# One pair's fourth weight sum in its own tile, and a residual prepared by accumulating transfers, in a Trainium2 encoder trunk

## Chip, cores and metric

The kernel runs on one core of one Trainium2 chip. The metric is the device time of one execution in microseconds (us); smaller is better. The engines are called PE (TensorE), DVE (VectorE), ACT (ScalarE), POOL (GpSimd) and SP (SyncE). SP issues the weight loads from memory, POOL issues the transfers that add one tile of the on-chip memory to another, and works little otherwise.

## What is computed

Two requests of 512 and 256 tokens, 768 tokens of 1024 values, run through two layers with shared weights. Each layer is a feed-forward block (FFN), a token mixer and a second FFN; the first layer's mixer is a gated linear recurrence, the second's a windowed attention. A last normalisation ends the trunk. The part that matters here is the FFN, run four times (f0, f1 around the first mixer, f2, f3 around the second):

```python
def swiglu_ffn(x, w1, w2):              # x [768,1024], w1 [1024, 2 x 2816], w2 [2816,1024]
    gate, up = jnp.split(x @ w1, 2, axis=-1)
    return (jax.nn.silu(gate) * up) @ w2

x = x + 0.5 * swiglu_ffn(rmsnorm(x, g), w1, w2)
```

All data are float32.

## The kernel before

**Storage and precision.** x stays on chip in six tiles of 128 tokens by 1024 values; the first three are the token half 0, the last three half 1. A float32 operand is split into a high and a low part: ACT copies it into the matmul's rounded format (the high part), and DVE subtracts that from the original (the low part). A product is three matmuls, high by high, high by low, low by high. The weights are split so at L225 (ACT) and L226 (DVE), activations at L369 and L370.

**Seven products.** A pair of 128 columns of the gate matrix and the 128 of the up matrix is treated as a 2 x 2 block matrix: a11 and a12 are the upper and lower half of the gate columns, a21 and a22 those of the up columns; the tokens are the two halves. As in the Strassen-Winograd scheme seven products p1 to p7 take the place of eight, with sums of weights on one side (for p7: a21 + a11; for p3 the sum of all four blocks) and sums of activations s1 to s4 on the other. The activation sums are made on DVE by `first_sum` and `up_sums` (L503, L511). The down projection works the same way, and its results are added to x by `add_x` (L792).

**The residual trick.** The down products of a block are combined so that x can take them directly. For that the residual is prepared once per FFN: with x12, x22 the left and right half of a token block in half 1, and x21 the right half of the block in half 0, x12 += x22 and x21 -= x22. Before, that is six DVE operations (L720 and L721, three each) in `down_quad`, at the first group only, anywhere behind the last sum. They are undone at the end, in `down_last`.

**The opening.** f0 starts with two plain pairs. f1, f2 and f3 start with one plain pair (pair 0, two halves of tokens), woven with the *opened pair*, pair 1, whose products run in the order p7, p3, (plain half 1), p1, p2, p6, p5, p4, in `opened_pair` (L671). p7 needs s1 and p3 needs plain activations only, so both can start before half 1 is normalised and turned. PE meanwhile turns the normalised token blocks (L435), and ACT evicts what PE turned (L446).

**Weights.** `quad_steps` (L195) loads a pair's two raw tiles (`wr`, four buffers of 512 KB) and one block more into an `s3` tile (two buffers of 256 KB), adds a11 to that tile and a22 to a21 by accumulating transfers (`into`, L155, issued by POOL), and stages the seven weights in an order, here `OPEN`: p1, p2, p7, p3, p6, p5, p4. In an opened pair two more sums follow in place: *second* (a11 += a21) behind p1's split, and *fourth* (a12 += a11) behind p2's split and the landing of second. p3's weight is a12 after fourth. SP and POOL work through their transfers in the order of the program; a transfer that waits keeps all behind it.

Of the kernel before, what the change touches and what calls it, by code (L numbers as in the profile page):

```python
# [12 lines left out]
AF = mybir.ActivationFunctionType  # L13
# [3 lines left out]
P = 128  # L17
# [18 lines left out]
HB = H // P  # L36
PLAIN = {"f0": 2, "f1": 1, "f2": 1, "f3": 1}
# [8 lines left out]
OPEN = ("p1", "p2", "p7", "p3", "p6", "p5", "p4")  # L46
# [11 lines left out]
class Trunk:  # L58
    def __init__(self, ctx, tc, consts):
        self.tc, self.nc = tc, tc.nc  # L60
        pool = lambda name, **kw: ctx.enter_context(tc.tile_pool(name=name, bufs=1, **kw))
        self.cp = pool("consts")
        self.xp = pool("xp")
        self.wp = pool("wp")
        self.tp = pool("tp")
        self.sp = pool("stats")
        self.ap = pool("arena")
        self.pp = pool("psum", space=bass.MemoryType.PSUM)
        self.dp = pool("dram", space=bass.MemoryType.DRAM)
        self.uid = 0  # L70
        self.deferred = []
        self.queue, self.loaded, self.staged, self.held = [], [], {}, 0
        self.more = {}
        self.shut = False
        self.setup(consts)

    def name(self, s):
# [119 lines left out]
    def quad_steps(self, key, raws, srcs, order):  # L197
        nc = self.nc
        flat = lambda t: t.rearrange("p a b -> p (a b)")
        up = len(raws) == 2  # L200
        if up:
            a11, a12, a21, a22 = (flat(t[:, h : h + 4, :]) for t in raws for h in (0, 4))
            three = [srcs[1].rearrange("(k p) c -> p k c", p=P)[:, :4, :]]
        else:
            a11, a12, a21, a22 = (flat(t) for t in raws)
            three = [srcs[2][:, i : i + 1, :] for i in range(2)]
        spare = up and (PLAIN[key[0]] == 2 or key[1] > 2)
        s3 = []
        for i, src in enumerate(three):
            t = self.wp.tile([P, 512], F32, tag="s3", name=self.name("s3"), bufs=2)  # L210
            self.last_load = nc.sync.dma_start(t.rearrange("p (a b) -> p a b", a=src.shape[1]), src)
            self.into(t, a11[:, i * 512 : (i + 1) * 512])
            s3.append(t)
        self.into(a21, a22)

        def split(name, srcs, eng=None):
            if up:
                w = self.wtile()
                hi, lo = w[:, :512], w[:, 512:]
            else:  # L220
                hi, lo = self.wtile(), self.wtile()
            n = srcs[0].shape[-1]
            for i, src in enumerate(srcs):
                h, l = (t[:, i * n : (i + 1) * n] for t in (hi, lo))
                nc.scalar.copy(h, src)  # L225
                (eng or nc.vector).tensor_sub(l, src, h.bitcast(F32))  # L226
            view = lambda t: t.rearrange("p (a b) -> p a b", a=4 if up else 2)
            self.staged[(*key, name)] = (view(hi), view(lo), 1 if up else 2)

        own = {"p1": [a11], "p2": [a12], "p3": [a12], "p4": [a22], "p5": [a21], "p6": [a11], "p7": s3}  # L230
        pin = self.tc.keep_in_program_order
        add = {"second": lambda: nc.vector.tensor_add(a11, a11, a21), "fourth": lambda: nc.vector.tensor_add(a12, a12, a11)}  # L232
        before = {} if up else {"p6": "second", "p3": "fourth"}
        behind = {"p5": "second", "p4": "fourth"} if up else {}

        if order == OPEN:
            add = {"second": lambda: self.into(a11, a21), "fourth": lambda: self.into(a12, a11)}
            behind, pin = {"p1": "second", "p2": "fourth"}, lambda ins: None

        def step(name):  # L240
            if name in before:
                pin(add[before[name]]())
            split(name, own[name], nc.gpsimd if spare and name == "p5" else None)
            if name in behind:
                pin(add[behind[name]]())

        gated = lambda i: order == OPEN and i >= GATED
        return [(1 if up else 2, lambda name=name: step(name), gated(i)) for i, name in enumerate(order)]
# [240 lines left out]
    def sums(self):  # L489
        tiles = lambda kp: [self.tn[(i // 2, i % 2)][:, kp] for i in range(4)]  # L490
        third = [tiles(kp)[3] for kp in range(2)]
        for kp, t in enumerate(third):
            self.nc.vector.tensor_sub(t, tiles(kp)[1], t)
        for name, out, x, y in (("t1", 1, 0, 1), ("t2", 0, 0, 3), ("t4", 2, 2, 0)):
            for kp in range(2):
                t = tiles(kp)
                self.nc.vector.tensor_sub(t[out], t[x], t[y])
                self.put(name, kp, t[out])
        for kp, t in enumerate(third):
            self.put("t3", kp, t)  # L500
        self.last_sum = self.last_lo

    def first_sum(self):  # L503
        for kp in range(2):
# [6 lines left out]
    def up_sums(self):  # L511
        add, sub = self.nc.vector.tensor_add, self.nc.vector.tensor_sub
        for name, op, out, x, y in (
            ("s2", sub, (1, 0), (1, 0), (0, 1)),
            ("s3", sub, (0, 0), (0, 1), (0, 0)),
            ("s4", add, (1, 1), (1, 1), (1, 0)),
        ):
            for kp in range(2):
                t = self.tn[out][:, kp]
                op(t, self.tn[x][:, kp], self.tn[y][:, kp])  # L520
                self.put(name, kp, t)
        self.last_sum = self.last_lo

    def spill_factors(self):
        self.kept = {}
        for name in ("t3", "t2", "t1", "t4"):
            for kp in range(2):
                t = self.kept[(name, kp)] = self.dp.tile([P, 4 * H], F32, name=self.name("kept"))
                self.nc.gpsimd.dma_start(t, self.ops[(name, kp)].bitcast(F32).rearrange("p a b c -> p (a b c)"))
# [60 lines left out]
    def gated(self, pss, act=None, dve=None):  # L590
        t = self.tmp(H)
        with self.tc.issue_after(act) if act else nullcontext():
            self.nc.scalar.activation(t, pss[0], AF.Silu)
        with self.tc.issue_after(dve) if dve else nullcontext():
            self.nc.vector.tensor_mul(t, t, pss[1])
        return t
# [116 lines left out]
    def down_quad(self, tag, g, hid):  # L713
        nc = self.nc
        cols = lambda b, c: self.x[b][:, c * 512 : (c + 1) * 512]
        if g == 0:
            with self.tc.issue_after(self.last_sum):
                for i in range(HB):
                    x12, x21, x22 = cols(HB + i, 0), cols(i, 1), cols(HB + i, 1)
                    nc.vector.tensor_add(x12, x12, x22)  # L720
                    nc.vector.tensor_sub(x21, x21, x22)  # L721
        banks = {}
        for name in DOWN:
            wh, wl = self.take((tag, "down", g, name))
            chain = {"p2": "p1", "p4": "p5", "p3": "p7"}.get(name, name)
            for i in range(HB):
                if name == chain:
                    banks[(chain, i)] = self.ps()
                ps = banks[(chain, i)]
                sl = slice(i * P, (i + 1) * P)  # L730
                for kp in range(2):
                    h = hid[FACTOR[name]]
                    a, w = (h[:, kp, 0, sl], h[:, kp, 1, sl]), (wh[:, kp, :], wl[:, kp, :])
                    for q, (x, y) in enumerate(((0, 0), (0, 1), (1, 0))):
                        nc.tensor.matmul(  # L735
                            ps,
                            a[x],
                            w[y],
                            start=name == chain and kp == 0 and q == 0,
                            stop=kp == 1 and q == 2,  # L740
                            skip_group_check=True,
                        )
                x22 = cols(HB + i, 1)
                dst = {"p2": cols(i, 0), "p4": cols(i, 1), "p3": cols(HB + i, 0)}.get(name, x22)
                self.add_x(dst, ps, -0.5 if name in ("p1", "p5") else 0.5)
            self.done((tag, "down", g, name))
# [1004 lines left out]
```

## Time and profile before

| What | us |
|---|---|
| three runs | 2758.54, 2761.22, 2761.22 |
| median | 2761.22 |
| the profiled execution | 2758.39 |
| its span, first to last instruction | 2756.5 |
| f1's opening, roughly | 1005 to 1055 |
| f2's opening | 1500 to 1570 |
| f3's opening | 2250 to 2335 |

The rest of the page: the mean granted clock of TensorE over the span is 0.999. The transfers moved 334.41 MB, 121 GB/s in the mean. A row of the timeline gives the start, the time, the engine, the source line and operation, the kind of tile written and read, the shapes, the count of equal neighbours, and in brackets the engine's idle time before it with what released it. A row of the chain of waits gives a start, a time and what ran then on the path that ended last. Neighbouring matmuls overlap: one starts before the one ahead has ended. An ACT cast whose source is `wr` or `s` splits a weight; one whose source is `big` or `tA` splits an activation.

### The profile page before, as it was taken

To read this page: it belongs to the slowest core of one execution; us is meant where nothing else is said; L and a number is where in the kernel's file an instruction comes from. 1 tells how busy PE (TensorE), PEld (TensorE's weight loads), DVE (VectorE), ACT (ScalarE), POOL (GpSimd) and SP (SyncE) were. 2 spreads that over 40 slices of the span, in tenths; PEclk is the share of its full clock that TensorE was granted. 3 is DMA by queue.
4 is the path that set the end of the run, shared out by engine and by line. 5 is a ranking of instruction groups with operands and counts; after the bars stand their busy time and mean duration, and the time that the engine had idled before them with its cause. 6 is when DMAs were issued, how large, how long until landed. Compare 5 with 4: busy or idle time off the path is not lost.

```text
span 2756.5 us, 41004 instructions
## 1 busy us (share of the span) xinstructions
PE 2731.8 (99%) x15045; PEld 2538.8 (92%) x15045; DVE 2199.7 (80%) x3802; ACT 1404.4 (51%) x2645; POOL 459.0 (17%) x516
## 2 busy tenths in 40 slices
PE   8999999999999999999999999999999999999998
PEld 8999999989999889999998999999888889999997
DVE  8788788768887889788878977887847869788877
ACT  6444444634455675444455643444458855444443
POOL 1111121200000110211121121112005621211120
PEclk9999999999999999999999999999999999999999
DMA  6554556741122744655555365545424434655453
GB/s 171 133 127 113 124 144 166 226 140 39 39 61 64 203 121 100 145 134 125 119 135 130 92 146 133 126 118 138 130 73 114 87 65 98 144 134 130 119 130 111
DMA packets 358362, 334.41 MB, mean 121 GB/s; under 512 B 14904, under 2 KB 273424, under 8 KB 358160
## 3 DMA queue, kind: packets, MB, share of 16 engines
q1 hardware_dynamic: 305328, 226.40, 27.9%
q0 software_dynamic: 48528, 91.90, 19.2%
q10 hardware_dynamic: 4304, 13.49, 1.4%
q8 instruction: 118, 1.93, 0.3%
q14 instruction: 84, 0.69, 0.1%
HBM read 227.66 MB, written 15.73 MB: 88 GB/s over the span
## 4 chain that ended last, share of the span: by engine, by line
PE 91%; DVE 4%; ACT 2%; DMA 1%; issue 1%; POOL 0%; DVEq 0%; ACTq 0%; POOLq 0%
PE ps L626 41%; PE ps L735 16%; PE ps L768 6%; PE ps L949 6%; PE ps L364 5%; PE ps L365 5%; PE ps L366 5%; PE ps L1012 3%; DVE big L370 1%; PE ps L1117 1%; DVE w L226 1%; PE ps L1605 1%; DMA wr<-wr 1%; PE ps L435 1%; PE ps L1093 1%
## 5 line engine op out<-in xcount | busy, mean ns | idle before, releaser
L626 PE MATMUL ps<-big,w 128*128 128x384 f32 x6972 | 1214.2, 334 | 2.9 <-ACT w L225 2.4
L626 PEld LDWEIGHTS ps<-big,w 128*128 128x128 f32 x6972 | 1209.3, 188 | 5.3 <-ACT w L225 2.7
L225 ACT CAST w<-wr 128x512 fp32r<-128x512 f32 (+1 forms) x618 | 430.5, 704 | 665.7 <-PE ps L626 315.3
L226 DVE TENSOR_TENSOR w<-wr,w 128x512 fp32r<-128x512 f32 (+1 forms) x541 | 435.2, 808 | 143.1 <-ACT w L225 121.8
L735 PE MATMUL ps<-w,big 128*128 128x512 f32 x2016 | 461.1, 390 | 0.2 <-DVE x L796 0.2
L735 PEld LDWEIGHTS ps<-w,big 128*128 128x128 f32 x2016 | 376.6, 188 | 80.6 <-ACT big L369 2.7
L155 POOL DMA_DIRECT2D s<-wr x129 | 113.6, 887 | 1248.0 <-DVE wr L232 362.4
L796 DVE SCALAR_TENSOR_TENSOR x<-ps,x 128x512 f32<-128x512 f32 x420 | 273.1, 683 | 12.8 <-PE ps L768 12.4
L370 DVE TENSOR_TENSOR big<-tA,big 128x384 fp32r<-128x384 f32 x308 | 190.3, 629 | 20.5 <-ACT big L369 20.3
L155 POOL DMA_DIRECT2D wr<-wr x118 | 104.0, 881 | 549.7 <-DVE big L370 152.1
L369 ACT CAST big<-tA 128x384 fp32r<-128x384 f32 x308 | 152.7, 514 | 81.2 <-DVE tA L667 30.4
L364 PE MATMUL ps<-big,w 128*128 128x384 f32 x544 | 187.5, 345 | 0.8 <-ACT w L191 0.8
L365 PE MATMUL ps<-big,w 128*128 128x384 f32 x544 | 183.1, 337 | 0.1
L366 PE MATMUL ps<-big,w 128*128 128x384 f32 x544 | 182.7, 336 | 0.0
L949 PE MATMUL ps<-w,big 128*128 128x512 f32 x756 | 178.1, 393 | 0.1
L768 PE MATMUL ps<-w,big 128*128 128x512 f32 x756 | 174.6, 391 | 0.9 <-DVE x L796 0.9
L768 PEld LDWEIGHTS ps<-w,big 128*128 128x128 f32 x756 | 141.0, 188 | 31.0 <-DVE x L796 2.1
L949 PEld LDWEIGHTS ps<-w,big 128*128 128x128 f32 x756 | 140.3, 188 | 28.9 <-DVE w L370 0.6
L226 POOL TENSOR_TENSOR w<-wr,w 128x512 fp32r<-128x512 f32 x77 | 111.7, 1451 | 104.5 <-ACT w L225 102.0
L232 DVE TENSOR_TENSOR wr<-wr,wr 128x512 f32<-128x512 f32 (+1 forms) x120 | 109.8, 915 | 0.0
L654 DVE TENSOR_TENSOR tA<-tA,ps 128x384 f32<-128x384 f32 x80 | 44.0, 550 | 81.0 <-PE ps L626 81.0
L364 PEld LDWEIGHTS ps<-big,w 128*128 128x128 f32 x544 | 102.3, 188 | 1.3 <-ACT w L191 1.1
(234 smaller groups left out, 3691.7 us busy)
## 6 DMA issues: line engine op xcount, KB each, us to landing
wr<-in_ffn_w_dram SPq DMA_DIRECT2D x256, 512.0 KB, 4.0
s<-wr POOLq DMA_DIRECT2D x129, 256.0 KB, 4.7
s<-in_ffn_w_dram SPq DMA_DIRECT2D x123, 256.0 KB, 3.2
wr<-wr POOLq DMA_DIRECT2D x89, 256.0 KB, 4.1
wr<-in_hg_w_in_dram SPq DMA_DIRECT2D x32, 512.0 KB, 3.9
wr<-wr POOLq DMA_DIRECT2D x29, 512.0 KB, 4.6
spill<-x ACTq DMA_DIRECT2D x12, 512.0 KB, 3.9
kept<-big POOLq DMA_DIRECT2D x8, 768.0 KB, 6.5
```

The lines of the kernel that those rows point to most:

```text
L155: self.nc.gpsimd.dma_start(out, src, accum_op=ALU.add)
L225: nc.scalar.copy(h, src)
L226: (eng or nc.vector).tensor_sub(l, src, h.bitcast(F32))
L364: nc.tensor.matmul(out, a[0], b[0], start=first, stop=False)
L365: nc.tensor.matmul(out, a[0], b[1], start=False, stop=False)
L366: nc.tensor.matmul(out, a[1], b[0], start=False, stop=last)
L370: self.last_lo = self.nc.vector.tensor_sub(lo, src, hi.bitcast(F32)).ins
L626: self.nc.tensor.matmul(ps, a[x], b[y], start=first and k == 0 and i == 0, stop=k == 3 and i == 2, skip_group_check=True,)
L735: nc.tensor.matmul(ps, a[x], w[y], start=name == chain and kp == 0 and q == 0, stop=kp == 1 and q == 2, skip_group_check=True,)
L768: nc.tensor.matmul(ps, a[x], w[y], start=name == chain and k == 0 and q == 0, stop=k == 2 and q == 2, skip_group_check=True,)
L796: self.nc.vector.scalar_tensor_tensor(x, ps, c, x, ALU.mult, ALU.add)
L949: nc.tensor.matmul(ps, x[:, sl], y, start=fresh and k == 0 and q == 0, stop=k == 3 and q == 2, skip_group_check=True,)
```

## The change

Two things change in f1, f2 and f3; f0 and the mixers keep their code.

1. The opened pair gets a second `s3` tile. It is loaded with a12, a11 is added to it, and then a21 once a22 has been added to that. p3 takes its weight from this tile. The transfer *fourth* is gone; *second* stays. Both `s3` buffers are now taken by the opened pair, until p7 and p3 have been split.
2. `up_sums`, right behind s2, calls a new `prepare`: for each of the three token blocks an ACT copy with the factor -1 makes -x22 in a scratch tile, and two accumulating transfers do x12 += x22 and x21 += -x22. `down_quad` does its DVE work in f0 only.

```diff
-            three = [srcs[1].rearrange("(k p) c -> p k c", p=P)[:, :4, :]]
+            part = lambda i, k: srcs[i].rearrange("(k p) c -> p k c", p=P)[:, k : k + 4, :]
+            three = [part(1, 0)] + ([part(0, 4)] if order == OPEN else [])
...
-            self.into(t, a11[:, i * 512 : (i + 1) * 512])
+            self.into(t, a11 if up else a11[:, i * 512 : (i + 1) * 512])
             s3.append(t)
         self.into(a21, a22)
+        if order == OPEN:
+            self.into(s3[1], a21)
...
         if order == OPEN:
-            add = {"second": lambda: self.into(a11, a21), "fourth": lambda: self.into(a12, a11)}
-            behind, pin = {"p1": "second", "p2": "fourth"}, lambda ins: None
+            own.update({"p3": s3[1:], "p7": s3[:1]})
+            add = {"second": lambda: self.into(a11, a21)}
+            behind, pin = {"p1": "second"}, lambda ins: None
...
                 self.put(name, kp, t)
+            if name == "s2" and self.joined:
+                self.prepare()
         self.last_sum = self.last_lo
+        self.joined = True
+
+    def prepare(self):
+        cols = lambda b, c: self.x[b][:, c * 512 : (c + 1) * 512]
+        neg = self.big([P, HB, 512])
+        for i in range(HB):
+            x12, x21, x22 = cols(HB + i, 0), cols(i, 1), cols(HB + i, 1)
+            self.nc.scalar.activation(neg[:, i], x22, AF.Copy, scale=-1.0)
+            self.into(x12, x22)
+            self.into(x21, neg[:, i])
...
-        if g == 0:
+        if g == 0 and PLAIN[tag] == 2:
```

`joined` is False until `up_sums` has run for the first time, which is in f0.

How the instructions move is told at three places. The first is POOL in f1, from the opened pair's first accumulation on. Before (1278 is p7's tile, 1276 holds a11 and a12, 1277 a21 and a22, 1313 to 1315 belong to pair 2, 1357 to 1359 to pair 3):

```order
L155 DMA s3_1278_8967<-wr_1276_8963 128x512
L155 DMA wr_1277_8965<-wr_1277_8965 128x512
L155 DMA s3_1315_9208<-wr_1313_9204 128x512
L155 DMA wr_1314_9206<-wr_1314_9206 128x512
L155 DMA wr_1276_8963<-wr_1277_8965 128x512
L155 DMA wr_1276_8963<-wr_1276_8963 128x512
L155 DMA s3_1359_9475<-wr_1357_9471 128x512
```

and now (1279 is p3's tile, 1314 to 1316 are pair 2's, 1359 to 1361 pair 3's, 1245 to 1247 the three x tiles of half 1, 1230 an x tile of half 0, 1352 the scratch tile):

```order
L155 DMA s3_1278_8967<-wr_1276_8963 128x512
L155 DMA s3_1279_8970<-wr_1276_8963 128x512
L155 DMA wr_1277_8965<-wr_1277_8965 128x512
L155 DMA s3_1279_8970<-wr_1277_8965 128x512
L155 DMA wr_1315_9210<-wr_1315_9210 128x512
L155 DMA x_1245_8771<-x_1245_8771 128x512
L155 DMA x_1246_8773<-x_1246_8773 128x512
L155 DMA wr_1276_8963<-wr_1277_8965 128x512
L155 DMA x_1247_8775<-x_1247_8775 128x512
L155 DMA s3_1316_9212<-wr_1314_9208 128x512
L155 DMA s3_1361_9488<-wr_1359_9484 128x512
L155 DMA x_1230_8685<-big_1352_9430 128x512
```

The two sums into p3's own tile come ahead of everything, fourth (`wr_1276<-wr_1276`) is gone, and pair 2's p7 sum has moved from ahead of second to behind it.

The second place is ACT in f1, where p7's weight is split. Before, from p7's cast (w_1325) to p3's (w_1326):

```order
L225 CAST w_1325_9283<-s3_1278_8967 128x512
L446 ACTIVATE big_1329_9309<-ps_1328_9305,cols_92 128x384
L446 ACTIVATE big_1329_9309<-ps_1330_9311,cols_92 128x384
L446 ACTIVATE big_1329_9309<-ps_1331_9316,cols_92 128x384
L446 ACTIVATE big_1329_9309<-ps_1332_9321,cols_92 128x384
L369 CAST big_1333_9326<-big_1329_9309 128x2x384
L369 CAST big_1334_9329<-big_1329_9309 128x2x384
L446 ACTIVATE big_1336_9345<-ps_1335_9341,cols_92 128x384
L446 ACTIVATE big_1336_9345<-ps_1337_9347,cols_92 128x384
L446 ACTIVATE big_1336_9345<-ps_1338_9352,cols_92 128x384
L225 CAST w_1326_9286<-wr_1276_8963 128x512
```

and now:

```order
L228 CAST w_1326_9286<-s3_1278_8967 128x512
L228 CAST w_1327_9289<-s3_1279_8970 128x512
L450 ACTIVATE big_1330_9312<-ps_1329_9308,cols_92 128x384
L450 ACTIVATE big_1330_9312<-ps_1331_9314,cols_92 128x384
L450 ACTIVATE big_1330_9312<-ps_1332_9319,cols_92 128x384
L450 ACTIVATE big_1330_9312<-ps_1333_9324,cols_92 128x384
```

p3's cast has moved up over nine instructions and stands ahead of the first evictions. Further on, behind s2's first halves, ACT now has the three copies (the second of s2's casts ahead, s3's and s4's casts behind, then p4's weight, pair 2's p1 weight and the eviction of plain half 1's bank, once L686, now L701):

```order
L373 CAST big_1351_9427<-big_1306_9181 128x2x384
L535 ACTIVATE big_1352_9430<-x_1245_8771 128x512
L535 ACTIVATE big_1352_9430<-x_1246_8773 128x512
L535 ACTIVATE big_1352_9430<-x_1247_8775 128x512
L373 CAST big_1353_9441<-big_1295_9129 128x2x384
L373 CAST big_1354_9445<-big_1295_9129 128x2x384
L373 CAST big_1355_9449<-big_1337_9348 128x2x384
L373 CAST big_1356_9453<-big_1337_9348 128x2x384
L228 CAST w_1358_9481<-wr_1277_8965 128x512
L228 CAST w_1362_9492<-wr_1314_9208 128x512
L701 COPY tA_1364_9496<-ps_1363_9495 128x384
```

The three L535 rows are new there; all behind them stood in the same order before.

The third place is DVE in f2, where a later pair's results are put together (L658 to L667), before:

```order
L721 TENSOR_TENSOR x_1230_8685<-x_1230_8685,x_1245_8771 128x512
L658 TENSOR_TENSOR tA_2016_14106<-tA_2016_14106,ps_2013_14103 128x384
L226 TENSOR_TENSOR w_2024_14206<-wr_1987_13939,w_2024_14206 128x512
L659 TENSOR_TENSOR tA_2018_14108<-ps_2014_14104,tA_2016_14106 128x384
L662 TENSOR_TENSOR tA_2017_14107<-tA_2017_14107,tA_2016_14106 128x384
L660 TENSOR_TENSOR tA_2018_14108<-tA_2018_14108,ps_2012_14102 128x384
L665 TENSOR_TENSOR tA_2016_14106<-tA_2016_14106,ps_2015_14105 128x384
L720 TENSOR_TENSOR x_1246_8773<-x_1246_8773 128x512
L721 TENSOR_TENSOR x_1231_8687<-x_1231_8687,x_1246_8773 128x512
L667 TENSOR_TENSOR tA_2017_14107<-tA_2016_14106,tA_2017_14107 128x384
```

and now:

```order
L673 TENSOR_TENSOR tA_2020_14126<-tA_2020_14126,ps_2017_14123 128x384
L229 TENSOR_TENSOR w_2028_14226<-wr_1991_13959,w_2028_14226 128x512
L674 TENSOR_TENSOR tA_2022_14128<-ps_2018_14124,tA_2020_14126 128x384
L677 TENSOR_TENSOR tA_2021_14127<-tA_2021_14127,tA_2020_14126 128x384
L675 TENSOR_TENSOR tA_2022_14128<-tA_2022_14128,ps_2016_14122 128x384
L680 TENSOR_TENSOR tA_2020_14126<-tA_2020_14126,ps_2019_14125 128x384
L682 TENSOR_TENSOR tA_2021_14127<-tA_2020_14126,tA_2021_14127 128x384
```

The residual's operations are gone from between the others, whose order is the same.

More of the change, by code (lines that the diff above doesn't have):

```diff
@@ L73, in __init__ @@
         self.more = {}
-        self.shut = False
+        self.shut = self.joined = False
         self.setup(consts)
@@ L500, in sums @@
             self.put("t3", kp, t)
-        self.last_sum = self.last_lo
     def first_sum(self):
```

## Prediction

> **What bounds the kernel now.** I read the page's busy table first, then the windows around the openings of the second, third and fourth FFN (called f1, f2, f3 after their tags; f0 is not changed), then waits, timelines and chain there.
>
> ```profile
> PE 2731.8 (99%) x15045; PEld 2538.8 (92%) x15045; DVE 2199.7 (80%) x3802; ACT 1404.4 (51%) x2645; POOL 459.0 (17%) x516
> 1005.00:1055.00 50.00, 47.62 (x268) 43.52 (x267) 42.38 (x62) 42.30 (x76) 5.21 (x6) 1.00 0.39 90
> 1500.00:1570.00 70.00, 69.87 (x406) 67.28 (x405) 65.51 (x102) 49.17 (x89) 10.90 (x11) 1.00 0.50 113
> 2250.00:2335.00 85.00, 84.13 (x471) 78.97 (x470) 73.64 (x121) 56.65 (x105) 9.59 (x10) 1.00 0.38 85
> 1055.00:1300.00 245.00, 245.00 (x1297) 229.78 (x1296) 202.78 (x334) 106.00 (x185) 42.43 (x43) 1.00 0.55 130
> ```
>
> TensorE (PE) is busy for 99% of the span, so only what makes PE wait is worth anything. The change adds and removes no matmul. In the window rows (length, then busy time of PE, PEld, DVE, ACT, POOL) PE lacks 2.38 us in f1's opening, 0.13 in f2's, 0.87 in f3's, and nothing in the steady part behind f1's opening. The whole gain must come out of those few microseconds, plus the little that PE loses on either side of a wait. The granted clock (third from the end) is 1.00 in all four.
>
> The loss in f1 is one wait, and what leads to it is short (timeline of PE, then two pieces of the chain of waits, then ACT's timeline):
>
> ```profile
> 1034.41 2.24 PE L626 MATMUL ps<-big,w 128*128 128x384 f32 x12
> 1039.04 0.62 PE L626 MATMUL ps<-big,w 128*128 128x384 f32 x2 [2.38 <-ACT w L225]
> 1030.78 3.28 DMA wr<-wr
> 1034.70 3.65 DMA wr<-wr
> 1038.37 0.62 ACT L225 CAST w<-wr 128x512 fp32r<-128x512 f32 x1 [2.02 <-DMA wr<-wr]
> 1117.87 58.26 PE ps L626 x336
> ```
>
> The 12 matmuls are product p7 of the opened pair, the next two begin p3. p3's weight is a12+a11+a21+a22, made in place by two accumulating transfers one behind the other (second, then fourth): 3.28 and 3.65 us, then the ACT cast. Matmuls of this shape are issued every 0.173 us (58.26 for 336), so p7 has issued at 1034.41 + 12 x 0.173 = 1036.49, and PE stands until 1039.04: 2.55 us, 0.17 more than the row's idle, since a matmul's end lies behind the next one's start. The two that start again take 0.62 instead of 0.17 + 0.33. f1 loses 2.55 + 0.12 = **2.67 us** here.
>
> **The change part by part.**
>
> *p3's own tile.* p3's sum no longer hangs on the two late transfers. The new tile gets a12 by a load, then a11, then a21 (to which a22 has been added). How early, and where its cast will stand:
>
> ```profile
> 1009.21 0.86 POOL L155 DMA_DIRECT2D wr<-wr  x1 [7.04 <-DMA wr<-in_ffn_w_dram]
> s<-wr POOLq DMA_DIRECT2D x129, 256.0 KB, 4.7
> 1030.55 0.65 ACT L225 CAST w<-s 128x512 fp32r<-128x512 f32 x1
> 1031.47 2.00 ACT L446 ACTIVATE big<-ps,cols 128x384 f32<-128x384 f32 x4 [0.27 <-PE ps L435]
> 1047.36 1.14 ACT L225 CAST w<-wr 128x512 fp32r<-128x512 f32 x2
> ```
>
> f1's transfer a21+=a22 was issued at 1009.21; with 3.65 to land, as above, and 4.7 for the last sum the tile is ready at 1017.6. ACT now casts it right behind p7's cast of 1030.55, 13 us later, so the 2.67 go. Not quite all: two such casts take 1.14 us, so each has an ACT slot of 0.52, and this one now stands ahead of the four evictions of 1031.47, for which PE's last transposes wait. p7's slot ends at 1031.07, so 0.40 of the 0.52 falls into the gap before 1031.47, and 0.12 is late; with none of the gap usable 0.52. I take 0.2, nearer to the first. In f2 and f3 the same cast is put ahead of evictions too; PE's timeline showed no wait for them, so nothing is charged, with 0.5 each as the upper bound. **f1: -2.47.**
>
> In f2 and f3 PE already ran p7 and p3 unbroken. There p3's weight was late for ACT and DVE alone:
>
> ```profile
> 1523.68 0.62 ACT L225 CAST w<-wr 128x512 fp32r<-128x512 f32 x1 [1.74 <-DMA wr<-wr]
> 2274.74 0.62 ACT L225 CAST w<-wr 128x512 fp32r<-128x512 f32 x1 [2.48 <-DMA wr<-wr]
> 2275.39 0.69 DVE L226 TENSOR_TENSOR w<-wr,w 128x512 fp32r<-128x512 f32 x1 [1.88 <-ACT w L225]
> 2280.70 0.34 PE L364 MATMUL ps<-big,w 128*128 128x384 f32 x1
> 2281.37 0.34 PE L366 MATMUL ps<-big,w 128*128 128x384 f32 x1
> ```
>
> ACT idles 1.74 and 2.48 us, f3's DVE 1.88, and both then work up a queue for which PE waits soon after: from 2280.70 to 2281.37 two steps take 0.67 instead of 0.35, since the low half of an operand comes late from DVE. With 1.88 us given back to DVE that goes. **f3: -0.32.**
>
> *The residual by transfers.* 18 DVE operations go (L720, L721, three of each in f1, f2 and f3). What PE lost later in the openings, and the removed operations ahead of it on DVE:
>
> ```profile
> 1561.70 4.49 PE L626 MATMUL ps<-big,w 128*128 128x384 f32 x23
> 1550.20 0.60 DVE x L720
> 1560.20 0.60 DVE x L721
> 2317.19 1.49 PE L626 MATMUL ps<-big,w 128*128 128x384 f32 x7 [0.47 <-ACT tA L643]
> 2302.59 0.68 DVE L720 TENSOR_TENSOR x<-x 128x512 f32<-128x512 f32 x1
> 2312.60 0.68 DVE L721 TENSOR_TENSOR x<-x,x 128x512 f32<-128x512 f32 x1
> 2332.20 2.08 PE L735 MATMUL ps<-w,big 128*128 128x512 f32 x8 [0.21 <-DVE x L796]
> L720 DVE TENSOR_TENSOR x<-x x12: 676/679/684, 51.8 to 2319.4; 128x512 f32<-128x512 f32 x12
> ```
>
> f2: 23 matmuls should take 22 x 0.173 + 0.33 = 4.14 and take 4.49, 0.35 more. ACT's eviction for them comes late behind a DVE queue that had no gap, with two removed operations in it, 0.60 us each: 1.2 us given back, more than is lost. **f2: -0.35.** f3, at 2317.19: 0.47 of idle and the 0.17 that hides beside it, and seven matmuls in 1.49 instead of 1.37: 0.76, again behind two removed operations. **f3: -0.76.** At 2332.20: 0.21 + 0.17 and about 0.1 to restart, 0.48. The last removed operations ended 12 us earlier (L720's last start is 2319.4), and DVE had a gap in between; it goes only if what leads to that wait moves further than PE does. I take half. **f3: -0.24.**
>
> *The added ACT work.* Three copies per opening make -x22. No row shows them; between the slot and the duration of an ACT cast of as many elements (0.52, 0.62) they cost 1.6 to 1.9 us. The ACT wait removed ahead of them covers that: 2.02, 1.74, 2.48. They stand ahead of the eviction (L686) that frees the bank for the second half of plain half 1:
>
> ```profile
> 1048.40 0.48 ACT L686 COPY tA<-ps 128x384 f32<-128x384 f32 x1
> 1051.63 2.59 PE L626 MATMUL ps<-big,w 128*128 128x384 f32 x14
> 2288.85 0.48 ACT L686 COPY tA<-ps 128x384 f32<-128x384 f32 x1
> 2289.39 2.89 PE L626 MATMUL ps<-big,w 128*128 128x384 f32 x15
> ```
>
> In f1 2.75 us lie between the bank's release and its use. ACT moves up by 2.02 - 1.57 = 0.45 and PE by 2.47, so 0.7 stay. In f3 0.06 lie between; ACT moves up by 2.48 - 1.57 = 0.9 and PE by 0.32, so 0.65 stay. Without the cover f1 would pay 1.3 and f3 1.5. I take 0, since every one of the three rows covers the lower cost.
>
> The six transfers themselves are off every engine that PE waits for, bar POOL's issues. Before, DVE did this work as late as 2319.4 and nothing waited; the new ones stand right behind s2, some 30 us earlier in f3. Cost 0; landing would have to take longer than that for a price.
>
> *The buffer.* p3's tile takes the second s3 buffer, so pair 2's load and sum start only when the opened pair's p7 has been split. In the old order pair 3's load stood at that point:
>
> ```profile
> 1034.01 0.37 SPq L211 DMA_DIRECT2D s<-in_ffn_w_dram  x1
> 1048.78 0.63 ACT L225 CAST w<-s 128x512 fp32r<-128x512 f32 x1
> DMA to landing us min/median/max: 2.5/3.2/6.7
> DMA to landing us min/median/max: 2.5/4.4/9.9
> ```
>
> Pair 2's cast is due at 1048.78 less the 0.45 that ACT moves up, 14.3 us after the load's issue at 1034.01. The last two rows are the landings of the line that loads these tiles (L211) and of the line that accumulates (L155). Load and sum need 3.2 + 4.7 = 7.9 by the medians. Cost 0, with 6.4 us to spare; the longest landings, 6.7 and 9.9, would make 16.6, 2.3 too late.
>
> **Sum:** 2.47 + 0.35 + 0.32 + 0.76 + 0.24 = 4.1 us. The profiled execution took 2758.39, so 2754.3; the median of the runs is 2761.22, 2.83 above it, which gives **2757**, 0.15% less. A measurement of this kernel can tell about 0.2% (5.5 us) from no change.
>
> **The rivals.**
>
> *DVE gains nothing, and only f1's stall goes.* More issues on POOL may slow DVE:
>
> ```profile
> L417 DVE TENSOR_SCALAR big<-x,stat x36: 743/752/920, 8.2 to 2269.6; 128x1024 f32<-128x1024 f32 x36
> 1497.49 0.92 DVE L417 TENSOR_SCALAR big<-x,stat 128x1024 f32<-128x1024 f32 x1
> 1497.32 1.18 POOL L155 DMA_DIRECT2D s<-wr  x1 [26.57 <-ACT stat L415]
> ```
>
> The slowest L417 of 36 (0.92 against a median of 0.75) overlaps an issue that took 1.18, where the one at 1009.21 took 0.86. Seven more issues in an opening, at 0.17 each, are 1.2 us, as much as is given back ahead of the waits of f2 and f3. Then 2761.2 - 2.5 = 2758.7. Against it: DVE's work there is nearly all TENSOR_TENSOR, whose L720 row hardly spreads (676 to 684 ns). Chance 0.17.
> [...]
>
> *The own tile is late, or ACT finds no cover.* A late tile needs 13 us more than worked out, and then nothing goes: 2761. With no cover for the copies f1 gives back 1.3 and f3 1.5: 2757.1 + 2.8 = 2760. Chance of both 0.1.
>
> *Slower.* Pair 2's p7 weight comes later than its cast; ACT stands, then PE, in all three openings. It decides from a landing 14.3 us after the release, and each microsecond beyond costs 3. At the longest landings 2.3 us each: 2757 + 7 = 2764, 0.1% slower. Over 0.2% it is from 3.2 in each opening, a landing 17.5 after the release: 2767 and more. Chance 0.08 in all, 0.05 beyond 0.2%.
>
> *More than 0.2%.* All that stands in the openings closes (0.44 more than the sum), and the run comes out at the lower of the times seen (2758.54, 2761.22): 2754. Chance 0.19.
>
> The forecast has the remaining 0.46. Range 2751.5 to 2762.5: from the lower of the times less 7 (the sum, the 0.44, and 2.5 for losses that I do not see and that DVE's freed time may close) to just short of the slower case. Chances: faster by over 0.2% 0.2, within 0.75, slower 0.05.
>
> **What would show it.** p7 and p3 in f1 as one row of matmuls without a wait; the ACT waits on `wr<-wr` gone from all three openings; f2's 23 matmuls back at 4.14; no wait on L643 at f3's 2317. The forecast is wrong if PE waits on L686's bank, if a cast `w<-s` of pair 2 waits for a transfer, or if DVE's rows grow longer.

## The result and the profile after

| | before | changed |
|---|---|---|
| median of 9 runs, us | 2760.19 (2758.54 to 2761.87) | 2752.79 (2751.44 to 2753.83) |
| the profiled execution | 2758.39 | 2753.83 |
| its span | 2756.5 | 2752.0 |

The ratio is 0.9972, 95% interval [0.9962, 0.9983]. A second set gave 2753.32 against 2759.31, 0.9977 [0.9967, 0.9987]. So the change is worth 6.0 to 7.4 us, 0.23 to 0.28%; 4.1 us (0.15%) was forecast, and the range of 2751.5 to 2762.5 holds the result.

The page and the windows of the changed kernel, to be set beside the rows in the prediction (busy time of PE, PEld, DVE, ACT, POOL behind the length):

```profile
PE 2730.4 (99%) x15045; PEld 2538.4 (92%) x15045; DVE 2191.9 (80%) x3784; ACT 1409.2 (51%) x2654; POOL 477.1 (17%) x537
1005.00:1055.00 50.00, 50.00 (x281) 45.81 (x280) 44.16 (x65) 44.66 (x82) 10.53 (x12) 1.00 0.61 122
1500.00:1570.00 70.00, 69.94 (x409) 67.85 (x408) 61.68 (x95) 51.34 (x92) 15.09 (x17) 1.00 0.65 141
2250.00:2335.00 85.00, 84.86 (x477) 80.45 (x476) 73.42 (x118) 57.49 (x104) 14.38 (x15) 1.00 0.46 103
```

PE is busy throughout f1's opening (47.62 of 50 before) and all but throughout f3's (84.13 of 85 before). DVE is busy for 7.8 us less, ACT for 4.8 us more, POOL for 18 us more. The matmuls are as many as before. The timeline of the changed kernel at the places that the prediction named, first PE, then ACT, then POOL (start, time, engine, line, operation, count, idle before):

```profile
1035.48 4.33 PE L641 MATMUL ps<-big,w 128*128 128x384 f32 x24
1560.83 5.36 PE L641 MATMUL ps<-big,w 128*128 128x384 f32 x30
2313.78 6.40 PE L641 MATMUL ps<-big,w 128*128 128x384 f32 x36
2328.82 5.43 PE L750 MATMUL ps<-w,big 128*128 128x512 f32 x23
1031.65 1.17 ACT L228 CAST w<-s 128x512 fp32r<-128x512 f32 x2
1032.69 2.03 ACT L450 ACTIVATE big<-ps,cols 128x384 f32<-128x384 f32 x4
1044.49 1.67 ACT L535 ACTIVATE big<-x 128x512 f32<-128x512 f32 x3
1040.12 0.86 POOL L155 DMA_DIRECT2D s<-wr  x1 [5.92 <-DVE big L374]
```

p7 and p3 are one row of 24 matmuls, which take 23 x 0.173 + 0.33 = 4.31 when nothing is lost. f2's 30 and f3's 36 are whole rows too (29 and 35 steps of 0.173 and 0.33 are 5.35 and 6.39), and the last wait, on L796 in f3, is gone with the others. The two casts, p7's and p3's, stand side by side, and the evictions follow at once.

The two programs run the same 15045 matmuls, in all but the same order, so the start of the n-th matmul in one trace can be taken from its start in the other. The differences, summed over the stages (us gained on the first trace of before, counted from the first matmul; a median over 20 neighbours at each boundary, 1020, 1060, 1490, 1580, 1990, 2245 and 2340 in the old trace):

| trace | up to f1 | f1 | rest of f1 | f2 | rest of f2 | attention | f3 | rest | sum |
|---|---|---|---|---|---|---|---|---|---|
| changed | -1.15 | 2.57 | -0.24 | 0.33 | -0.03 | 0.92 | 1.69 | 0.11 | 4.2 |
| changed, second trace | -1.19 | 2.61 | -0.13 | 0.33 | -0.10 | 0.86 | 1.72 | 1.10 | 5.2 |
| before, second trace | -0.45 | 0.00 | -0.05 | -0.11 | 0.06 | -0.13 | 0.36 | 0.14 | -0.2 |
| before, third trace | 0.49 | -1.43 | -0.04 | -0.57 | 0.03 | 0.19 | 0.19 | 0.15 | -1.0 |

The openings give 2.57, 0.33 and 1.69, where 2.47, 0.35 and 1.32 were forecast. The rest of the timed gain had to be found.

### The profile page after: what moved, and what is told of

It reads as the page before. It is cut to its first block, busy times and chain, and to the rows that moved or that the text cites. A ratio compares the mean times of both kernels' runs of the same rounds, so it can differ in the third digit from the quotient of the medians.

```text
span 2752.0 us, 41062 instructions
## 1 busy us (share of the span) xinstructions
PE 2730.4 (99%) x15045; PEld 2538.4 (92%) x15045; DVE 2191.9 (80%) x3784; ACT 1409.2 (51%) x2654; POOL 477.1 (17%) x537
## 4 chain that ended last, share of the span: by engine, by line
PE 80%; DVE 1%; ACT 1%; DMA 1%; issue 0%; SPq 0%; DVEq 0%; POOL 0%; ACTq 0%; POOLq 0%
PE ps L641 33%; PE ps L750 13%; PE ps L964 6%; PE ps L783 5%; PE ps L368 5%; PE ps L369 5%; PE ps L370 5%; PE ps L1027 3%; PE ps L1132 1%; PE ps L439 1%; PE ps L1620 1%; PE ps L1108 1%; PE ps L1632 0%; PE ps L1582 0%; PE ps L1633 0%; PE ps L1583 0%
```

## The experiments

Ratios are to the kernel before, timed on the same chip in the same set. The median of before was 2759.31 for the first four kernels, 2759.55 for the next four, 2759.15 for the three after them.

### The kernel before and the changed kernel once more

No edit.

> The kernel before, once more, profiled on its own. Nine runs of it spread from 2758.54 to 2761.87, and the execution whose trace was read took 2758.39, the lowest of all. Theory H1 (the wait for p3's weight in f1 is longer in most executions than in the one read): the new trace, if it takes 2760 or more, has over 2.67 us lost between p7 and p3, and the rest of the trace agrees with the old one within 0.5 us. Rival H2 (the spread is made elsewhere, in the recurrence, the attention or at the start): the loss between p7 and p3 is 2.67 within 0.3, and the difference lies outside 1005 to 1055.

> The changed kernel once more, on the same chip as the others. Theory: ratio 0.9965 to 0.998 again, PE without a wait in all three openings. If the sum of the two parts alone is larger than this, they overlap in f2 and f3, where either gives DVE more than PE lost; if it is equal, each part has its own share.

Before: 2758.84, ratio 1.0 [0.9991, 1.0008], traced in 2758.51. Changed: 2753.32, ratio 0.9977 [0.9967, 0.9987], traced in 2752.56. The second trace of before agreed with the first in f1 to 0.01 us, so it could not say where the slower executions of before lose their time; it settled neither theory. The two traces of the changed kernel agree in every opening to 0.04 us.

### Each part alone

The own tile alone:

```diff
-            if name == "s2" and self.joined:
-                self.prepare()
...
-        if g == 0 and PLAIN[tag] == 2:
+        if g == 0:
```

> p3's own tile alone; the residual stays with DVE. Theory: f1's loss of 2.67 goes (less 0.2), and so does the 0.32 of f3, 2.8 us in all; since ACT's and DVE's waits go here too (1.6 to 1.9 us of DVE in f2 and f3), f2's 0.35 and f3's 0.76 may go as well: between 2.8 and 4.1 us faster in the trace, ratio 0.9985 to 0.999 if the typical run is like the traced one. With H1 the timed gain is larger than the traced one, 5 us or more (ratio 0.998). Rival (the DVE operations are what f2 and f3 need): f2's 23 matmuls still take 4.49 and the wait on the eviction at 2317 in f3 stays.

The residual alone is the second half of the change (`prepare`, its call and the condition in `down_quad`) put into the kernel before.

> The residual by transfers alone; p3's weight is made by second and fourth as before. Theory: f1's loss of 2.67 stays; f2's 0.35 and f3's 0.76 go, since 1.2 us of DVE work ahead of them is gone; the three ACT copies have no removed wait to cover them, so in f3 the eviction that frees plain half 1's bank comes 1.5 us late: between 1.1 us faster (copies hidden all the same) and 0.4 us slower. Rival (the transfers are what made the change larger than forecast): 3 us or more faster.

The own tile alone: 2753.30, ratio 0.9978 [0.9969, 0.9987], as fast as both parts. The residual alone: 2765.74, ratio 1.0023 [1.0014, 1.0032], **6.4 us slower**. The parts don't add: one gives everything, the other harms unless the first is there. By stages:

| trace | f1 | f2 | f3 |
|---|---|---|---|
| own tile alone | 2.71 | 0.34 | 1.75 |
| residual alone | -2.45 | -2.62 | -2.57 |

In the own tile's trace f2's and f3's later losses are gone although DVE still does its eighteen operations there: the DVE idle that ended with p3's wait was relief enough. The rival that these operations were what f2 and f3 needed falls.

The residual alone went far beyond what was expected (at most 0.4 us slower). Its timeline, PE's waiting rows and then POOL in f1:

```profile
1040.28 0.98 PE L638 MATMUL ps<-big,w 128*128 128x384 f32 x2 [3.29 <-ACT w L225]
1528.75 2.75 PE L638 MATMUL ps<-big,w 128*128 128x384 f32 x12 [0.80 <-ACT w L225]
1543.07 3.25 PE L638 MATMUL ps<-big,w 128*128 128x384 f32 x17 [1.16 <-ACT tA L698]
2296.35 4.98 PE L638 MATMUL ps<-big,w 128*128 128x384 f32 x18 [2.16 <-ACT tA L698]
...
1030.74 0.86 POOL L155 DMA_DIRECT2D x<-x  x1 [4.04 <-DVE w L226]
1031.50 1.00 POOL L155 DMA_DIRECT2D wr<-wr  x1
1032.07 1.32 POOL L155 DMA_DIRECT2D x<-x  x1
1036.26 0.86 POOL L155 DMA_DIRECT2D wr<-wr  x1 [2.87 <-DVE big L370]
```

Two waits are on p3's weight (L225), in f1 and f2, and two on the eviction that frees plain half 1's bank (L698, before the change L686). In POOL's rows an x12 transfer stands right ahead of second (the first `wr<-wr`) and another right behind it; fourth (the last row) is issued 4.76 us behind second, where it was 3.92 before (1030.78 and 1034.70). Its row names an operation of DVE as what ended POOL's idle time, but fourth waits for second to land, and that was at 1035.62, 0.64 us ahead of the issue, as in the kernel before (1034.06 and 1034.70).

### What in the residual costs

Four kernels take it apart. x12 += x22 by transfers, x21 -= x22 left with DVE, old weight:

```diff
-            self.nc.scalar.activation(neg[:, i], x22, AF.Copy, scale=-1.0)
             self.into(x12, x22)
-            self.into(x21, neg[:, i])
...
+        if g == 0:
...
+                    if PLAIN[tag] == 2:
+                        nc.vector.tensor_add(x12, x12, x22)
                     nc.vector.tensor_sub(x21, x21, x22)
```

> p3's weight by second and fourth as before; of the residual only x12 += x22 goes to transfers, x21 -= x22 stays with DVE, so there are no ACT copies. In the run with the whole residual and the old weight the loss against before was 2.5 us in f1 and 1.5 in f2 at p3, then 1.5 in f2 and 3.8 in f3 at the eviction L698. Theory: the two at p3 come from the x12 transfers, which stand ahead of second and beside fourth in POOL's queue, and the two at L698 from the ACT copies. Then here the losses at p3 stay (f1's idle 3.3 us, f2's 0.8) and those at L698 go: 2 to 4 us slower than before. Rival (the copies cause all of it): not slower, up to 1 us faster.

2761.95, ratio 1.0012 [1.0003, 1.0021]: 2.4 us slower. f1 loses 2.55 as with the whole residual, f3 nothing: the waits at L698 are gone. f2's loss of 2.71 is as large as there but made up otherwise: all but 0.3 of it now stands at p3, whose wait grew from 0.80 to 1.75 us, where 0.8 was expected. The rival falls.

The same with the three transfers behind second and fourth:

```diff
+                    if PLAIN[tag] == 2:
+                        nc.vector.tensor_add(x12, x12, x22)
+                    else:
+                        nc.vector.tensor_copy(x22[:, :1], x22[:, :1])
+                        self.into(x12, x22)
```

> The same, but each x12 transfer waits for an operation of DVE behind the last sum (a copy of one column of x22 onto itself), so that all three stand behind second and fourth in POOL's queue. Theory: the waits at p3 are those of before again (2.4 us in f1, none in f2), the time is that of before or up to 1 us less. Rival (transfers cost through the traffic, not through their place): as slow as the run with the early x12 transfers.

2759.46, ratio 1.0001 [0.9992, 1.001]: the time of before, with PE's wait in f1 at 2.37 and none at p3 in f2. So three transfers cost by where they stand, ahead of second and fourth and landing beside them; the same bytes later cost nothing. Whether POOL's queue or the traffic beside the two sums holds these up was not separated: the edit moves both.

The whole residual, prepared behind s4 (`if name == "s4" and self.joined:`):

> The whole residual by transfers and the old weight, but prepared behind s4 instead of s2: on ACT the three copies now stand behind the eviction L698 and not ahead of it, and the x12 transfers stand ahead of second as in the run with the whole residual. Theory: the waits on L698 (1.2 us in f2, 2.2 in f3) go, the waits at p3 stay: 2 to 4 us slower than before, not 6.4. Rival (ACT's work as such is too much for the openings, wherever it stands): 5 us slower or more.

2762.27, ratio 1.001 [1.0001, 1.0019]: 2.7 us slower and no longer 6.4. f3's loss of 2.57 turns into a gain of 0.53, f1 and f2 lose as before (2.46, 2.32). So with the copies ahead of L698 the residual costs 3.7 us more, nearly all of it f3's 3.1, and what is left, 2.7, is the x12 transfers' part. In f2 the two can't be told apart so simply: there the wait at L698 goes, but p3's grows to 1.58. The landing of fourth in f2 shows why (chain of waits; before, the residual alone, x12 alone):

```profile
1519.03 4.63 DMA wr<-wr
1522.10 5.96 DMA wr<-wr
1521.49 6.90 DMA wr<-wr
```

It is 6.74 with the residual behind s4. In these three kernels two x12 transfers are issued right ahead of fourth.

And the changed kernel with every copy made twice:

```diff
             self.nc.scalar.activation(neg[:, i], x22, AF.Copy, scale=-1.0)
+            self.nc.scalar.activation(neg[:, i], x22, AF.Copy, scale=-1.0)
```

> The changed kernel with each negated copy made twice on ACT: 1.57 us more in each opening. In the changed kernel's trace the eviction L701 ended 0.0 (f1), 0.65 (f2) and 0.5 us (f3) ahead of its use. Theory (the cover of the copies is used up): PE waits on L701 about 1.5, 0.9 and 1.1 us, 3.5 in all; 3 to 4 us slower than the changed kernel, more if the clock drops behind a wait; ratio to before 0.999. Rival (other work of ACT can still give way): not over 1 us slower than the changed kernel.

2754.21, ratio 0.9982 [0.9973, 0.9991]: 0.7 to 0.9 us slower than the changed kernel (5.3 us faster than before in its set, where that was 6.0 faster; 0.9 between the two medians), not 3 to 4. The theory falls, and its rival holds. PE in f1 and the eviction, in the changed kernel and in this one:

```profile
1050.05 6.17 PE L641 MATMUL ps<-big,w 128*128 128x384 f32 x34
1050.04 0.47 ACT L701 COPY tA<-ps 128x384 f32<-128x384 f32 x1
1048.66 7.56 PE L642 MATMUL ps<-big,w 128*128 128x384 f32 x42
1050.22 0.47 ACT L702 COPY tA<-ps 128x384 f32<-128x384 f32 x1
```

PE goes on from 1048.66 without a wait (41 steps of 0.173 and 0.33 are 7.42, and the row takes 7.56), though the bank comes free at 1050.69 only. The order of PE's instructions shows why: before, p2's twelve matmuls stand first behind plain half 1; in the changed kernel three of p6's stand ahead of them, and with doubled copies all twelve. The order is fixed when the kernel is built, and with the copies other work was moved into the gap. Why that didn't happen for the residual alone in f2 and f3 is not shown. The trace of this kernel loses elsewhere: 0.85 us behind f1, where PE waits for an `add_x` on DVE (L812, at 1091), and 0.37 in f3.

### Where the own tile gives its gain

The own tile in f1 only (second and fourth stay in f2 and f3):

```diff
-        if order == OPEN:
+        alone = order == OPEN and key[0] == "f1"
+        if alone:
             self.into(s3[1], a21)
...
+        elif order == OPEN:
+            add = {"second": lambda: self.into(a11, a21), "fourth": lambda: self.into(a12, a11)}
+            behind, pin = {"p1": "second", "p2": "fourth"}, lambda ins: None
```

> The own tile in f1's opened pair alone; f2 and f3 keep second and fourth, and the residual stays with DVE everywhere. Theory (f1's stall is 2.5 us of the gain, f2 and f3 give 2.2 by DVE's and ACT's waits that go there, the rest is elsewhere): 2.5 to 3.5 us faster than before, ratio 0.9987 to 0.999; in the trace f2 and f3 lose what they lost before (about 0.4 and 1.6). Rival (f2 and f3 gain only because the work behind f1 falls in step differently): as fast as with the own tile in all three, 5.5 to 6 us.

2755.37, ratio 0.9988 [0.9979, 0.9997]: 3.8 us faster, slightly above the 2.5 to 3.5 expected; in the trace f1 gives 2.69, f2 -0.01 and f3 0.00. f3's wait is back:

```profile
2314.24 5.99 PE L644 MATMUL ps<-big,w 128*128 128x384 f32 x33 [0.51 <-ACT tA L661]
```

So f2 and f3 give 2.1 us of their own, and the rival (a mere change of step) falls.

p3's tile in the scratch pool, so that pair 2 has its buffer early:

```diff
+            if i and order == OPEN:
+                t = self.big([P, 512])
+            else:
+                t = self.wp.tile([P, 512], F32, tag="s3", name=self.name("s3"), bufs=2)
```

> The own tile in all three, residual with DVE, but p3's tile lies in the scratch pool, so that pair 2's load and sum have their s3 buffer as early as before the change. Theory (the late buffer costs nothing, the sum has several microseconds to spare): as fast as with both tiles in the s3 pool, 2753.3 within 1 us. Rival (the late load or its place in the queues costs a little in each opening): faster than that by 1 us or more.

2753.15, ratio 0.9978 [0.9969, 0.9987], as the own tile in the s3 pool. The late buffer costs nothing.

The changed kernel without copies (the first edit of the part before this one, made in the changed kernel):

> The changed kernel without the ACT copies: x12 += x22 by transfers, x21 -= x22 left with DVE as before. Theory (with p3 out of the way of second and fourth neither the early x12 transfers nor the copies cost anything, and DVE's relief is worth nothing more): the changed kernel's time, 2753.3 within 1 us. Rival (the copies still cost something, hidden in the sum of gains): faster by 1 us or more.

2753.85, ratio 0.998 [0.9972, 0.9989]: within 1 us of the changed kernel, as expected, though 0.7 above the kernel before this one, timed in the same set; a price of that size isn't ruled out. With p3 on its own tile, neither x12's transfers nor the copies have a larger one, and DVE's relief shows no value.

### The clock behind the wait

The late x12 transfers gave back the old wait (2.37), but that trace lost 1.56 us more in f1 than the first trace of before. Its rows, PE behind the wait and then the windows of 1 us (the granted clock is third from the end):

```profile
1040.15 0.62 PE L626 MATMUL ps<-big,w 128*128 128x384 f32 x2 [2.37 <-ACT w L225]
1041.13 0.52 PE L366 MATMUL ps<-big,w 128*128 128x384 f32 x1
1041.45 0.52 PE L364 MATMUL ps<-big,w 128*128 128x384 f32 x1
1040.00:1041.00 1.00, 0.85 (x4) 0.85 (x5) 0.87 (x2) 1.00 (x3) 0.00 (x0) 0.86 0.00 0
1041.00:1042.00 1.00, 1.00 (x5) 1.00 (x4) 1.00 (x2) 1.00 (x3) 0.00 (x0) 0.50 0.06 16
1042.00:1043.00 1.00, 1.00 (x4) 1.00 (x4) 1.00 (x2) 1.00 (x4) 0.00 (x0) 0.50 0.00 0
1043.00:1044.00 1.00, 1.00 (x4) 1.00 (x4) 1.00 (x3) 0.67 (x1) 0.00 (x0) 0.50 0.00 0
1044.00:1045.00 1.00, 1.00 (x7) 1.00 (x7) 0.90 (x2) 0.00 (x0) 0.00 (x0) 0.93 0.04 8
```

For some 3.4 us behind the wait the clock is 0.50, and a matmul is issued every 0.32 us instead of 0.173. Does that happen to the kernel before too? A last run, no edit:

> The kernel before, profiled a third time. In four runs with the old weight a wait at p3 in f1 was followed by some 3.3 us at half the TensorE clock, which costs 1.6 us more; in one of them the wait was no longer than before's own (2.37 us). In the two traces of before the clock stayed at 1.00. Theory (the half clock comes or not with the phase of the wait, and so in some executions of before): either the clock in 1041 to 1044 is 0.5, and then the time is 2759.5 or more, or it is 1.00 and the time 2758.5 or less. It is refuted by an execution of 2760 or more with the clock at 1.00 there and no other loss in the openings.

It took 2759.07, and its trace shows it (PE, then windows):

```profile
1038.31 1.01 PE L626 MATMUL ps<-big,w 128*128 128x384 f32 x2 [2.44 <-ACT w L225]
1038.00:1039.00 1.00, 0.69 (x2) 0.69 (x3) 0.71 (x2) 1.00 (x3) 0.00 (x0) 0.50 0.00 0
1039.00:1040.00 1.00, 1.00 (x4) 1.00 (x4) 1.00 (x2) 1.00 (x2) 0.00 (x0) 0.50 0.00 0
1040.00:1041.00 1.00, 1.00 (x4) 1.00 (x4) 1.00 (x2) 1.00 (x4) 0.00 (x0) 0.50 0.06 16
1041.00:1042.00 1.00, 1.00 (x6) 1.00 (x6) 1.00 (x2) 0.83 (x2) 0.00 (x0) 0.85 0.00 0
```

The same kernel, the same wait within 0.06 us, and f1 takes 1.43 us more than in its two other traces. The half clock came earlier than the window that the expectation named, and the time is 0.4 below its bound, since this execution was 0.49 ahead by f1. Seven traces have the old weight in f1. The clock dropped in one of the three of before (waits of 2.4 us), in the one with late transfers (2.37), and in all three whose wait was 3.3 us.

The phase can be read from the traces. Where windows of 1 us show both its ends, the half clock behind a wait lasted 3.40 to 3.42 us: in the late transfers' trace from 1040.72 to 1044.14 (the means 0.86 and 0.93 of the windows that it cuts give both ends), in that of x12 alone from 1040.94 to 1044.36, in that of the residual alone from 1040.34 to 1043.76 and from 2296.46 to 2299.86. These two falls lie 1256.12 us apart. In the traces of before and of the changed kernel the clock falls behind the last matmuls, at 2751.54 and 2750.18, and in both the trace's record of the clock is one stretch of 2737.49 us at 1.00 up to there, though the spans are 2756.5 and 2752.0. From these lengths an estimate: of all steps from 3.40 to 3.42 us only 3.4133 goes into 1256.12 and 2737.49 without a rest (368 and 802 times), so the changes of the clock are taken to lie on a grid of pieces of 3.4133 us. One fall, or one end of a half clock, then tells where the pieces of a trace lie (with the residual behind s4 PE's rows give the fall, where a matmul goes from 0.33 to 0.42 and 0.53 us behind 1041.50), and each wait can be divided by them (idle time as PE's rows give it; for the second trace of before no fall is shown):

| trace, place | wait | most idle time of PE in one piece | clock behind that piece |
|---|---|---|---|
| before, f1 | 2.38 | 1.39 | 1.00 |
| before, second, f1 | 2.37 | not shown | 1.00 |
| residual behind s4, f2 | 1.58 | 1.58 | 1.00 |
| x12 alone, f2 | 1.75 | 1.71 | 1.00 |
| before, third, f1 | 2.44 | 2.01 | 0.50 |
| x12 alone, f1 | 3.34 | 2.11 | 0.50 |
| residual behind s4, f1 | 3.27 | 2.15 | 0.50 |
| residual alone, f3 | 2.16 | 2.16 | 0.50 |
| late x12, f1 | 2.37 | 2.37 | 0.50 |
| residual alone, f1 | 3.29 | 3.29 | 0.50 |

The total wait doesn't order the rows, the idle time within one piece, so estimated, does in the nine that have it: from 2.01 us on the clock halved at the end of the piece, up to 1.71 it held. In the first traces of before and of the changed kernel no other wait of PE behind the first 15 us is over 1.1 us, and the clock falls behind none of them.

## Why the prediction was right, and what was mis-sized

- **f1's stall (2.47).** Right in mechanism and, against a trace at full clock, in size: 2.57. The cast ahead of the evictions cost little: 2.67 were lost, 2.57 came back. But the term was worked out from one execution whose clock held at 1.00. Where the clock drops behind the wait, 1.4 to 1.6 us more are lost (1.43 in the third trace of before, 1.56 in the late transfers'), and they go with the wait. The prediction read the clock as 1.00 in all its windows and had no term for this. It is the first piece of what the timed gain has over the forecast. How often it happens can't be counted from three traces. An estimate from the table of pieces: a wait of 2.4 us may stick out of a piece by 0.4 to 0.7 and still drop the clock, which is so for 53 to 71% of its positions ((3.41 - 2.4 + 0.8 to 1.4) / 3.41); if all are equally likely, that is 0.8 to 1.1 us in the mean.
- **f3 (1.32).** The three losses were rightly found; 1.69 came back. The half that was kept back at L796 came back whole, as did small losses that were not counted. f2's 0.35 was 0.33.
- **What earns f2's and f3's part.** Here a step failed: "The residual by transfers" was given f2's 0.35 and f3's 0.76 and 0.24. The own tile alone brings both, and the residual adds nothing to it. The forecast counted the relief of DVE once, so that the sum stands, but it put it down to the wrong part: that the sum came out owes something to luck, and of the two parts of the change one was worth the whole.
- **ACT's copies and their cover.** Costed at nothing in the changed kernel, and two kernels show no price that these runs can tell. But in f1 the zero didn't come by the forecast's way: 0.7 us were to stay between the bank's release and its use, and the bank came free at 1050.51 (1050.04 + 0.47), 0.46 behind the end of plain half 1's issue at 1050.05. Three of p6's matmuls, 0.52 us, fill that gap. Their price without cover was put at 1.3 in f1 and 1.5 in f3. Without cover f1 paid nothing and f3, through a wait of 2.16 and a clock at 0.5 behind it, 3.1 (2.57 lost where 0.53 is won with the copies later). That PE's order gives way, as in f1, was not thought of; in part the zero was luck.
- **The x12 transfers ahead of second.** The prediction named their place on POOL and gave it no price. With the own tile it has none that the runs can tell; with the old weight it is 2.4 us.
- **The buffer.** Right: pair 2's sum was issued at 1040.12 for a cast at 1050.41, and the early buffer changed nothing. The slower rival didn't come near.
- **DVE slowed by POOL's issues.** Not so. The slowest L421 (L417 before) of 36 took 0.755 us in the changed kernel, with 21 issues more. The slow pair at 1497 in the first trace of before has no like there.
- **The bound of 0.2%.** "Faster by over 0.2%" had a chance of 0.2 and is what came. The forecast of the traced difference was near (4.1 against 4.2 and 5.2 with all stages; the three openings alone gave 4.6, where 4.1 was meant for them), but the timed kernels differ by 6.0 to 7.4, and 2752.79 lies 4 us below the 2757 that was forecast. The range held it by the 2.5 us kept for losses not seen, not by a term that names them. Beside the clock, f2 loses 0.57 in the third trace of before, 0.40 of it at p3: there fourth took 5.13 us to land, not 4.63, and that goes with the own tile too. Another 0.5 to 1.0 us come from attention, where every kernel without a wait at p3 in f1 but one gains:

```profile
2209.53 0.54 PE L1372 MATMUL ps<-ident_r,s 128*128 128x128 f32 x4 [0.76 <-DVE s L370]
```

This wait in before (0.76, and 0.9 in its second trace) is 0.2 or nothing in both traces of the changed kernel. No instruction there is changed. The kernels with a longer wait in f1 gain there too (0.35 to 0.73), so it isn't tied to the gain in f1; why the work falls into step there stays open. Ahead of f1 both traces of the changed kernel lose some 1.2 us and the own tile alone nothing (0.06); the fourteen traces spread there from -1.2 to 0.5, the kernel with late x12 transfers at -0.95, so this can't be put down to the change. With the openings' 4.6, the clock's 0.8 to 1.1 and attention's 0.5 to 1.0 the account comes to 5.9 to 6.7 us, near the timed 6.0 and 7.4; the clock's share in it is an estimate.

## What to carry to other kernels

A weight that several products share in place is a chain: a sum of its own, made from what is there early, takes the chain off the path for one small load and one more buffer (of the 2.67 us that it cost in f1 here, 2.57 came back). Before moving work off a busy engine, look whether the same relief comes with a wait that goes anyway, and what the moved work stands ahead of in its new queue: here the same six transfers and three copies cost nothing, 2.7 or 6.4 us by what stood behind them. And judge a wait on TensorE by what the clock does behind it, in more than one trace: behind 2.4 us it held in two traces here and dropped in two.

## What the runs showed of the hardware

**The clock can drop behind a wait of 2.2 us, or hold behind one of 2.4.** It held behind 2.38 and 2.37 (before, two traces) and dropped behind 2.44 (before, third), 2.37 (late x12) and 2.16 (residual alone, f3), as the last one's windows show:

```profile
2297.00:2298.00 1.00, 1.00 (x4) 1.00 (x4) 1.00 (x2) 1.00 (x3) 0.00 (x0) 0.50 1.00 156
2300.00:2301.00 1.00, 1.00 (x8) 1.00 (x7) 0.00 (x0) 0.70 (x2) 0.00 (x0) 1.00 0.99 285
```

The three waits of 3.3 us in f1 all dropped it. In nine of the ten waits of the table above PE's idle time within one piece of the estimated grid of 3.4133 us sorts the outcomes: 2.01 and more dropped the clock, 1.71 and less did not. The half clock lasted 3.40 to 3.42 us in the four places where both its ends are shown, and a matmul was issued every 0.32 us in it instead of 0.173.

**Transfers beside a chain of transfers lengthen a link of it, not every one.** In f1, with an x12 transfer right ahead of second and one right behind it, second landed after 4.12 us and not 3.28, and fourth, which waits for that, was issued 4.76 us behind it and not 3.92. Fourth itself landed after 3.33, before after 3.65. In f2 fourth was issued right behind two x12 transfers, and it landed after 5.96 to 6.90 us, before after 4.63. Whether the queue or the traffic does that was not tried; with the three transfers later fourth was issued 3.93 behind second in f1 (1031.91 and 1035.84) and landed after 4.77 in f2.
